# A two-sequence hybrid encoder layer on one core: head by depth block, last products reordered, final scaling on GpSimd's queue

## The chip, the cores and the metric

The kernel runs on one core of a Trainium2 chip. The metric is the device time of one execution in microseconds, as a median over runs. The engines are named as in the profile: PE is TensorE's matmul, PEld its weight load, DVE VectorE, ACT ScalarE, POOL GpSimd, SP SyncE, which issues most transfers. A "q" behind an engine's name (SPq, POOLq) means its sequencer, for issues of transfers.

## The reference

Two inputs, a prompt of 512 tokens and a sample of 1024 tokens, of width 2048, pass the same layer with shared weights, everything in float32:

```python
def mixer_layer(x, norm_g, w_in, w_dw, b_dw, ln_g, ln_b, w_pw, sink, w_out):
    h = rms_norm(x, norm_g)
    z = h @ w_in                      # widths: val, glu, gate 1024 each, q 1024, k and v 256, gate 1024
    c_val, c_glu, c_gate, q, k, v, a_gate = jnp.split(z, split_points, axis=-1)
    ...
    conv_out = conformer_conv(c_val, c_glu, w_dw, b_dw, ln_g, ln_b, w_pw) * jax.nn.silu(c_gate)
    attn_out = banded_sink_attention(q, k, v, sink) * jax.nn.silu(a_gate)
    mix = jnp.concatenate([conv_out, attn_out], axis=-1) @ w_out
    return x + mix

def encoder(x, ...):
    x = mixer_layer(x, ...)           # one layer
    return rms_norm(x, final_norm_g)  # the final scaling spoken of here
```

The convolution has 31 taps over 1024 channels, the attention 8 heads of 128 with a band of one block of 128 to each side. `y_p` is the prompt's output, `y_s` the sample's.

## The kernel before

**Products.** Every large product is made of 128x512 matmuls in float32 with a reduced multiplier. An operand is split into a high part (a copy by ACT, L487) and a remainder (a difference by DVE, L488); three matmuls, high by high, high by remainder and remainder by high, make one product. The tiles of weights so split are `hl` (three buffers), their loads `raw` (three buffers of 512 KB), the tokens so split `t`. A weight tile needs 12 matmuls. Larger units are multiplied in seven block products in Strassen's manner (P1 to P7, over sums of blocks of tokens and of weights) instead of eight.

**Order.** The program is written as one stream on TensorE. After each few matmuls (`tick`) lanes of side work are advanced by a credit in time: each side job is a generator that yields the time that it is worth. A yielded number so sets how soon its next part is emitted and where it stands in the in-order queues of ACT, DVE and the transfers. `w_prep` prepares the next weight tiles ahead of the products.

**Head.** The very first unit (`Plain`, matmuls on L329) multiplies directly in eight steps: a half of the tokens, a half of the depth, and one of two columns of weights. Before it, SP loads four weight pieces of 512 KB for the halves of depth, and 8 tiles of x, halved in tokens. `token_sum` (L490 on ACT) splits x, with the norm's gain `norm_g`; `first_sums` goes through them.

**Last stage, from about 1932 us.** Two things run side by side. On TensorE the prompt's output product (`last_run`, L1762 for all but the last product, L1721 for the last): two column halves c, in each the seven products in the order P1 P2 P6 P5 P7 P3 P4 (`ALONE`), each over four weight tiles; two token blocks share a bank pair, so there are four blocks b of 128 rows. `tap` adds a product's bank into the rows (L1663). When one quarter of a block's row is complete (after P2, P7, P3, P4), `complete` squares it with a running sum on ACT (L1672) and multiplies it by the final gain on DVE (L1673). At a row's fourth quarter the root and its reciprocal follow (L681, L682), then four scalings of 128x512 by that row's number, in turn on DVE and ACT (L1688, L1686), and four stores of 256 KB into `y_p` (L1689). The second column half's rows of x and gains are loaded after the fourth product (`load_columns(1)`).

Beside it, a side job (`finish`) finishes the sample: for each half of the tokens it sums squares over the columns, takes the root, spreads the number over the partitions (L699, copied out on L1366); after both halves it goes over 16 blocks of 128 rows in `y_d`: loads one (even ones as one 128x1024 tile `f`, odd ones as two 128x512 tiles `p`, of which there are four), scales it on DVE (L1374) and stores it into `y_s` (L481). Loads are issued three blocks ahead; all its transfers are on SP's queue, where the weights' loads are, too. Accumulating transfers earlier in the kernel (L478) are those of GpSimd's queue.

Of the kernel before, what the change touches and what calls it, by code (L numbers as in the profile page):

```python
# [57 lines left out]
DIRECT = ("P1", "P2", "P3")  # L58
TURNS = ("P1", "P2", "P5", "P6", "P7", "P3", "P4")
# [240 lines left out]
class Plain(Unit):  # L300


    STEPS = [(0, 0, 0), (0, 0, 1), (0, 1, 0), (0, 1, 1), (1, 0, 0), (1, 0, 1), (1, 1, 0), (1, 1, 1)]

    def preps(self):
        self.raws = [self.e.raw_tile() for _ in range(2)]
        return [Prep(None, None) for _ in range(2)]

    def load_half(self, c, k):
        self.e.nc.sync.dma_start(self.raws[c][:, k], self.w[c][:, k * HALF : (k + 1) * HALF, :])  # L310

    def make_half(self, c, k):
        e = self.e
        t = e.hl[c] if c in e.hl else e.hl_tile()
        e.parts(t[:, 0, k], t[:, 1, k], self.raws[c][:, k])
        e.hl[c] = t
# [4 lines left out]
    def product(self, step, late):  # L321
        e, nc = self.e, self.e.nc
        t, k, c = self.STEPS[step]
        if k == 0:
            self.bank[t, c] = e.PS("abac"[2 * t + c], [W])
        acc, hl, toks = self.bank[t, c], e.hl[self.at[c]], e.T[f"A{t + 1}{k + 1}"]
        for j in range(HALF):
            for q, (l, r) in enumerate(((0, 0), (0, 1), (1, 0))):
                nc.tensor.matmul(  # L329
                    acc,  # L330
                    hl[:, l, k, j, :],
                    toks[j][:, r],
                    start=k == 0 and j == 0 and q == 0,
                    stop=k == 1 and j == HALF - 1 and q == 2,
                )
            if j == 0:
                for fn in late:
                    fn()
                if step >= 4:
                    e.w_prep(3 if step < 7 else 4)  # L340
                e.turn_over()
            e.tick(3 * MM)
        if step >= 6:
            e.hl.pop(self.at[c])
        for fn in self.after.get(step, ()):
            fn()
        return [lambda: e.urgently(self.tap, (t, c))] if k else []
# [60 lines left out]
class Encoder:  # L408
# [119 lines left out]

    def constants(self):
        nc, a = self.nc, self.a  # L530

        def load(key, shape):
            t = self.const.tile([P] + shape, F32, name="c_" + key)
            nc.sync.dma_start(t, a[key])
            return t

        self.norm_g = load("norm_g", [ND])
        self.norm_n = self.const.tile([P, ND], F32, name="norm_n")
        nc.vector.tensor_scalar(self.norm_n, self.norm_g, -1.0, None, ALU.mult)
# [3 lines left out]
        nc.vector.tensor_copy(self.ones_r, self.ones)  # L543

        def rest():
# [162 lines left out]
class Sequence:  # L708
# [64 lines left out]
    def first_sums(self, x):  # L773

        e, nc = self.e, self.e.nc
        col = lambda t, k: t[:, k : k + 1]
        for t in range(2):
            for k in range(2):
                for j in range(HALF):
                    self.token_sum(f"A{t + 1}{k + 1}", 0, j, x[j + k * HALF][:, t * W : t * W + W])  # L780
                yield
# [429 lines left out]
class Mix:  # L1211
# [128 lines left out]
    def finish(self):  # L1340
# [3 lines left out]
        def load(o):  # L1344
            if o >= ND:
                return
            if o % 2:
                ys = [e.PT("p", NP, [W]) for _ in range(2)]
                for t, y in enumerate(ys):
                    nc.sync.dma_start(y, self.y_d[o][:, t * W : t * W + W])  # L1350
            else:
                ys = [e.F([TS])]
                nc.sync.dma_start(ys[0], self.y_d[o])
# [4 lines left out]
        yield LOAD  # L1358
        for t in range(2):
            s = self.sv[:, t]  # L1360
            v = e.column_sums(s, W, 1.0 / D, RMS_EPS)
            r = e.small(NB)
            e.rsqrt(r, v, NB)
            yield S7
            ps = yield from e.spread(r, room=e.F)
            nc.scalar.activation(s, ps, AF.Copy)  # L1366
            yield 1000
        rb = self.sv.rearrange("p t n -> p (t n)")
        for o in range(ND):
            ys = held.popleft()  # L1370
            n = TS // len(ys)
            for t, y in enumerate(ys):
                cols = slice(t * n, t * n + n)
                nc.vector.scalar_tensor_tensor(y, y, e.fin_g[:, o : o + 1], rb[:, cols], ALU.mult, ALU.mult)  # L1374
                e.store(self.out[o][:, cols], y)
            load(o + 3)
            yield 2000
# [126 lines left out]
class LastPost(Post):  # L1504
# [90 lines left out]
    def last_weights(self):  # L1595
# [28 lines left out]
        for c in range(2):  # L1624
            for name in ALONE:
                for m in self.PAIRS:
                    self.place[c, name, m] = len(preps)
                    preps.append(one(c, name, m, c == 1 and name == ALONE[-1]))
# [36 lines left out]
    def complete(self, b, c, odd):  # L1665
# [7 lines left out]
        nc.vector.tensor_tensor(y, y, self.gain[c, odd], ALU.mult)  # L1673
# [5 lines left out]
        if n == 3:  # L1679
# [3 lines left out]
            for j in range(D // W):  # L1683
                y = self.column(self.rows[b], j)
                if j % 2:
                    nc.scalar.activation(y, y, AF.Identity, scale=r)  # L1686
                else:
                    nc.vector.tensor_scalar(y, y, r, None, ALU.mult)  # L1688
                nc.sync.dma_start(self.out[b * P : (b + 1) * P, j * W : (j + 1) * W], y)  # L1689
# [4 lines left out]
        "P7": ((1, 1),), "P3": ((0, 1),), "P4": ((1, 0),),  # L1694
# [4 lines left out]
    def tap(self, c, name, t, acc):  # L1699
        h, odd = self.ADDS[name][0]  # L1700
        self.add(2 * h + t, c, odd, acc)

    def last_run(self, at):
        e, nc = self.e, self.e.nc
        self.seen = {}
        tags = [{"P1": ("a", "a"), "P2": ("b", "c"), "P5": ("s", "s")}, {"P1": ("pt", "pv"), "P2": ("b", "c"), "P5": ("s", "s")}]
        pending = []
        step = 0
        for c in range(2):
            bank = [None] * 3  # L1710
            for name in ALONE:
                n = BANK[name]
                if name in FRESH:
                    bank[n] = [e.PS(tag, [W]) for tag in tags[c][name]]
                acc = bank[n]
                end = c == 1 and name == ALONE[-1]

                def products(t, m, i, part):
                    first, last = m == self.PAIRS[0] and i == 0, m == self.PAIRS[-1] and i == 1
                    for q, (x, l) in enumerate(self.PASSES):  # L1720
# [4 lines left out]
                            start=name in FRESH and first and q == 0,  # L1725
                            stop=name in LAST and last and q == 2,
# [24 lines left out]
                before = c == 1 and name == ALONE[-2]  # L1751
                for n, m in enumerate(self.PAIRS):
# [5 lines left out]
                    for i in range(2):  # L1758
                        for q, (x, l) in enumerate(self.PASSES):
                            for t in range(2):  # L1760
# [5 lines left out]
                                    start=name in FRESH and first and q == 0,  # L1766
                                    stop=name in LAST and last and q == 2,
# [6 lines left out]
                if step == 3:  # L1774
                    self.load_columns(1, e.F)
                step += 1
                done, pending = pending, []
                for t in range(2):
                    finished(t)
                for args in done:  # L1780
                    e.urgently(self.complete, *args)


def encoder(ctx, tc, a):
# [27 lines left out]
    def first():  # L1812
        x = [e.F([TS]) for _ in range(NF)] + [e.A([TS], F32)]
        part = lambda k, t: e.nc.sync.dma_start(x[k][:, t * W : t * W + W], sample.xT[k][:, t * W : t * W + W])
        for k in range(2):
            plain.load_half(0, k)
            for j in range(HALF):
                part(j + k * HALF, 0)
            plain.load_half(1, k)
# [3 lines left out]
        e.w_load(3)  # L1823
        sums = sample.first_sums(x)
        x = None
        for k in range(2):
            plain.make_half(0, k)
            next(sums)
            plain.make_half(1, k)
        next(sums)  # L1830
        next(sums)
        e.ready = 2
        plain.after[1] = [lambda: next(sums)]
# [239 lines left out]
```

## Time and profile before

| | |
|---|---|
| three runs | 2105.66, 2110.05, 2110.88 us, median 2110.05 |
| the profiled execution | 2105.98 us, of it span 2104.2 us |
| TensorE clock granted, mean | 0.995 |
| PE busy | 2062.6 us (98%), 9234 matmuls |
| DVE busy | 1752.5 us (83%) |
| ACT busy | 1042.7 us (50%) |
| POOL busy | 77.2 us (4%) |
| transfers | 494.53 MB, 235 GB/s over the span |

A timeline row has the start within the span, the duration, the engine, the line, the operation and its tiles (out<-in), and how many like it follow in a row; a bracket gives the idle time before it and what ended it. A row of waits has the engine, the tile and the line that waited, the tile and line that it waited for, then microseconds in total, times, and the longest. A group's row has the count, the busy time, the mean of one in ns, and the idle time before them. A row of transfers ends with count, size of one and microseconds from issue to landing.

### The profile page before, as it was taken

The numbers are of one execution on the slowest core, as the hardware profiler recorded it, in microseconds if no ns is written. First come the engines' busy times: TensorE is split into PE (matmuls) and PEld (weight loads), VectorE is DVE, ScalarE is ACT, GpSimd is POOL, SyncE is SP. The second block draws the span as 40 slices with busy tenths as digits, with TensorE's granted clock in tenths as the row PEclk, the third lists the DMA queues.
The fourth block names the chain that finished last, engine by engine and source line by source line (L and its number), as shares of the span: only waits on it lengthen the run. The fifth ranks groups of instructions, "written<-read, shape, count | busy, mean of one in ns | idle before, by whom it ended". The sixth has DMA issues, their size and how long they took to land.

```text
span 2104.2 us, 26927 instructions
## 1 busy us (share of the span) xinstructions
PE 2062.6 (98%) x9234; PEld 1693.9 (81%) x9234; DVE 1752.5 (83%) x2855; ACT 1042.7 (50%) x1682; POOL 77.2 (4%) x92
## 2 busy tenths in 40 slices
PE   8999999999999999999999999999999999999996
PEld 7878888888877888788888888887888888888885
DVE  8658798998899999999566777766799988899777
ACT  6476435333454444644455777336554343455444
POOL 0001110000001111100000000000000000000000
PEclk9999999999999999999999999999999999999998
DMA  8888887865577667954556555996689898677798
GB/s 283 305 290 248 204 216 229 292 206 171 179 230 191 171 168 180 274 162 150 160 174 188 175 180 188 318 333 208 234 286 302 280 328 286 212 263 269 250 311 308
DMA packets 248025, 494.53 MB, mean 235 GB/s; under 512 B 23248, under 2 KB 83024, under 8 KB 247888
## 3 DMA queue, kind: packets, MB, share of 16 engines
q1 hardware_dynamic: 235216, 469.74, 67.1%
q0 software_dynamic: 12672, 23.07, 6.9%
q8 instruction: 72, 1.18, 0.2%
q14 instruction: 65, 0.53, 0.1%
HBM read 331.77 MB, written 160.96 MB: 234 GB/s over the span
## 4 chain that ended last, share of the span: by engine, by line
PE 76%; DMA 9%; DVE 9%; issue 3%; ACT 2%; SPq 0%; POOL 0%; ACTq 0%; DVEq 0%; POOLq 0%
PE a L198 21%; PE a L632 13%; PE c L198 10%; PE c L632 6%; PE b L632 6%; PE b L198 5%; DVE hl L488 2%; PE pv L1145 2%; PE s L1116 2%; PE s L198 2%; PE a L1762 2%; DMA raw<-wsum_P 1%; PE pt L1150 1%; DMA f<-x_s 1%; PE s L1762 1%
## 5 line engine op out<-in xcount | busy, mean ns | idle before, releaser
L198 PE MATMUL a<-t,hl 128*128 128x512 f32 x2640 | 633.3, 391 | 8.1 <-ACT u L224 3.7
L198 PEld LDWEIGHTS a<-t,hl 128*128 128x128 f32 x2640 | 493.5, 188 | 115.6 <-ACT u L224 6.9
L487 ACT ACTIVATE hl<-raw 128x1024 fp32r<-128x1024 f32 (+1 forms) x356 | 324.1, 911 | 435.8 <-DVE raw L140 93.3
L488 DVE TENSOR_TENSOR hl<-raw,hl 128x1024 fp32r<-128x1024 f32 (+1 forms) x356 | 369.0, 1037 | 148.4 <-ACT hl L487 147.0
L632 PE MATMUL a<-t,hl 128*128 128x512 f32 x1344 | 329.7, 395 | 0.3 <-DVE hl L488 0.3
L198 PE MATMUL c<-t,hl 128*128 128x512 f32 x1320 | 320.8, 391 | 0.2
L198 PEld LDWEIGHTS c<-t,hl 128*128 128x128 f32 x1320 | 248.0, 188 | 53.3 <-ACT g L224 0.9
L632 PEld LDWEIGHTS a<-t,hl 128*128 128x128 f32 x1344 | 249.5, 189 | 50.8 <-DVE hl L488 0.7
L1000 DVE SCALAR_TENSOR_TENSOR f<-f,c_w_dw,f 128x512 f32<-128x512 f32 x248 | 174.9, 745 | 0.3
L632 PE MATMUL c<-t,hl 128*128 128x512 f32 x672 | 165.5, 394 | 0.0
L963 DVE SCALAR_TENSOR_TENSOR f<-f,c_w_dw,f 128x512 f32<-128x512 f32 x232 | 163.5, 743 | 1.7 <-ACT f L958 1.7
L632 PE MATMUL b<-t,hl 128*128 128x512 f32 x672 | 163.5, 392 | 0.2 <-DVE hl L488 0.2
L198 PE MATMUL b<-t,hl 128*128 128x512 f32 x660 | 160.0, 390 | 0.0
L632 PEld LDWEIGHTS b<-t,hl 128*128 128x128 f32 x672 | 124.9, 188 | 25.4 <-DVE hl L488 0.7
L632 PEld LDWEIGHTS c<-t,hl 128*128 128x128 f32 x672 | 125.1, 189 | 24.4
L198 PEld LDWEIGHTS b<-t,hl 128*128 128x128 f32 x660 | 123.7, 188 | 25.5
L992 DVE SCALAR_TENSOR_TENSOR f<-f,w_both,f 128x512 f32<-128x512 f32 x120 | 89.7, 748 | 1.8
L395 ACT ACTIVATE hl<-raw 128x1024 fp32r<-128x1024 f32 x44 | 46.5, 1056 | 61.2 <-PE a L632 23.6
L224 ACT ACTIVATE u<-a 128x512 f32<-128x512 f32 x82 | 48.6, 593 | 56.1 <-PE a L198 52.4
L224 ACT ACTIVATE g<-a 128x512 f32<-128x512 f32 x78 | 46.3, 593 | 59.1 <-PE a L198 53.9
L1130 ACT ACTIVATE p<-p,tiny 128x384 f32<-128x384 f32 (+1 forms) x96 | 54.6, 570 | 38.0 <-DVE tiny L1127 27.7
L487 ACT ACTIVATE a<-pt 128x512 fp32r<-128x512 f32 x64 | 38.0, 593 | 65.7 <-PE pt L1150 65.5
(332 smaller groups left out, 2562.0 us busy)
## 6 DMA issues: line engine op xcount, KB each, us to landing
raw<-w_in SPq DMA_DIRECT2D x171, 512.0 KB, 5.0
raw<-wsum_P SPq DMA_DIRECT2D x32, 512.0 KB, 4.9
raw<-w_out SPq DMA_DIRECT2D x31, 512.0 KB, 5.2
raw<-w_pw SPq DMA_DIRECT2D x24, 512.0 KB, 4.5
raw<-w_last SPq DMA_DIRECT2D x24, 512.0 KB, 5.3
wsum_P<-raw SPq DMA_DIRECT2D x47, 256.0 KB, 3.5
f<-x_s SPq DMA_DIRECT2D x16, 512.0 KB, 6.7
a<-sum_S SPq DMA_DIRECT2D x24, 256.0 KB, 6.0
```

The lines of the kernel that those rows point to most:

```text
L198: nc.tensor.matmul(acc, hl[:, l, o, j, :], toks[j][:, r], start=name in FRESH and j == 0 and q == 0, stop=name in LAST and j == HALF - 1 a ...
L224: nc.scalar.activation(t, bank, AF.Copy)
L395: e.nc.scalar.activation(t[:, 0], raw, AF.Copy)
L487: nc.scalar.activation(hi, x, AF.Copy)
L488: nc.vector.tensor_tensor(lo, x, hi.bitcast(F32), ALU.subtract)
L632: nc.tensor.matmul(job.acc[0], hl[:, l, kk // HALF, kk % HALF, :], r, start=i == 0 and p == 0, stop=i == nk - 1 and p == 2,)
L963: nc.vector.scalar_tensor_tensor(t, h[:, j : j + T], w(j), t, ALU.mult, ALU.add)
L992: nc.vector.scalar_tensor_tensor(m0, odd[:, j : j + H], both(j), m0, ALU.mult, ALU.add)
L1000: nc.vector.scalar_tensor_tensor(out, d[:, j : j + H], w(2 * j + k), out if j else m0, ALU.mult, ALU.add)
L1116: nc.tensor.matmul(ps[:, 0:n], qs[:, x, h], k[y][:, keys], start=p == 0, stop=p == 2)
L1130: nc.scalar.activation(p[:, 0:n], p[:, 0:n], AF.Exp, bias=nm[:, h : h + 1], accum_out=l[:, h : h + 1])
L1762: nc.tensor.matmul(acc[t], self.toks[name, m][:, x, i, t * P : (t + 1) * P], parts[i][l].rearrange("p a b -> p (a b)"), start=name in FRES ...
```

## The change

Four parts:

1. Head: the first unit runs through the depth block by block (a quarter of the depth for both columns in each of eight steps), its weights are loaded in pieces of one or three blocks between the x tiles, splits follow in the same order, and 16 small matmuls of 128x128 ones stand ahead of it (`warm`). `norm_n` is computed later.
2. `finish`: the sample's statistics are taken over all 1024 tokens in one pass, and both halves are spread directly behind one another. Loads and stores of the scaling are issued by GpSimd instead of SP; the yield between blocks is 5000 instead of 2000.
3. Last column half: the products go P1 P2 P6 P5 P3 P7 P4 (`ENDS`). P7 is added to two quarters there, and P4 is summed in banks of its own. The first block pair's rows are so complete after P3, the second's after P4. `complete` is emitted in the midst of the next product. `load_columns(1)` comes after the sixth product instead of the fourth.
4. Last scaling of a row: the fourth quarter isn't multiplied by the gain first; gain and row number go in at once (`scalar_tensor_tensor`), other quarters on ACT or DVE as before, and each row block is stored in two pieces of 512 KB instead of four of 256 KB.

```diff
+ENDS = (ALONE, ("P1", "P2", "P6", "P5", "P3", "P7", "P4"))
...
 class Plain(Unit):
-    STEPS = [(0, 0, 0), (0, 0, 1), (0, 1, 0), (0, 1, 1), (1, 0, 0), (1, 0, 1), (1, 1, 0), (1, 1, 1)]
+    STEPS = [(t, q) for t in range(2) for q in range(HALF)]
...
+    def load_some(self, c, k, j0=0, j1=HALF):
+        self.e.nc.sync.dma_start(self.raws[c][:, k, j0:j1], self.w[c][:, k * HALF + j0 : k * HALF + j1, :])
...
     def product(self, step, late):
+        t, quarter = self.STEPS[step]
...
+        for n in range(2):
+            i = 2 * quarter + n
+            k, j = divmod(i, HALF)
+            toks = e.T[f"A{t + 1}{k + 1}"]
+            for c in range(2):
+                acc, hl = self.bank[t, c], e.hl[self.at[c]]
+                for q, (l, r) in enumerate(((0, 0), (0, 1), (1, 0))):
+                    nc.tensor.matmul(acc, hl[:, l, k, j, :], toks[j][:, r], ...)
...
+    def warm(self):
+        ps = self.PS("pt", [P])
+        for _ in range(16):
+            self.nc.tensor.matmul(ps, self.ones_r, self.ones_r, start=True, stop=True)
...
     def finish(self):
...
-                    nc.sync.dma_start(y, self.y_d[o][:, t * W : t * W + W])
+                    nc.gpsimd.dma_start(y, self.y_d[o][:, t * W : t * W + W])
...
+        rb = self.sv.rearrange("p t n -> p (t n)")
+        v = e.column_sums(rb, TS, 1.0 / D, RMS_EPS)
+        r = e.small(2 * NB)
+        e.rsqrt(r, v, 2 * NB)
+        yield S7
         for t in range(2):
-            s = self.sv[:, t]
-            v = e.column_sums(s, W, 1.0 / D, RMS_EPS)
-            r = e.small(NB)
-            e.rsqrt(r, v, NB)
-            yield S7
-            ps = yield from e.spread(r, room=e.F)
-            nc.scalar.activation(s, ps, AF.Copy)
+            ps = yield from e.spread(r[:, t * NB : t * NB + NB], room=e.F)
+            nc.scalar.activation(self.sv[:, t], ps, AF.Copy)
             yield 1000
...
-                e.store(self.out[o][:, cols], y)
+                nc.gpsimd.dma_start(self.out[o][:, cols], y)
             load(o + 3)
-            yield 2000
+            yield 5000
...
     def complete(self, b, c, odd):
-        nc.vector.tensor_tensor(y, y, self.gain[c, odd], ALU.mult)
+        if n < 3:
+            nc.vector.tensor_tensor(y, y, self.gain[c, odd], ALU.mult)
...
+            for h in range(2):
+                other, last = (self.blocks(self.rows[b], h, o) for o in (1 - odd, odd))
+                nc.scalar.activation(other, other, AF.Identity, scale=r)
+                if h == c:
+                    nc.vector.scalar_tensor_tensor(last, last, r, self.gain[c, odd], ALU.mult, ALU.mult)
                 else:
-                    nc.vector.tensor_scalar(y, y, r, None, ALU.mult)
+                    nc.vector.tensor_scalar(last, last, r, None, ALU.mult)
+                nc.sync.dma_start(self.out[b * P : (b + 1) * P, h * half : (h + 1) * half], self.rows[b][h])
...
-        "P7": ((1, 1),), "P3": ((0, 1),), "P4": ((1, 0),),
+        "P7": ((1, 1), (1, 0)), "P3": ((0, 1),), "P4": ((1, 0),),
...
-                if step == 3:
+                    if n == 1:
+                        for args in pending:
+                            e.urgently(self.complete, *args)
+                        pending.clear()
+                if step == 5:
                     self.load_columns(1, e.F)
```

More of the change, by code (lines that the diff above doesn't have):

```diff
@@ L1624, in last_weights @@
         for c in range(2):
-            for name in ALONE:
+            for name in ENDS[c]:
                 for m in self.PAIRS:
                     self.place[c, name, m] = len(preps)
-                    preps.append(one(c, name, m, c == 1 and name == ALONE[-1]))
+                    preps.append(one(c, name, m, c == 1 and name == ENDS[c][-1]))
         return preps
@@ L1699, in tap @@
     def tap(self, c, name, t, acc):
-        h, odd = self.ADDS[name][0]
+        (h, odd), *more = self.ADDS[name]
         self.add(2 * h + t, c, odd, acc)
+        if c:
+            for h, odd in more:
+                self.add(2 * h + t, c, odd, acc)
     def last_run(self, at):
@@ L1710, in last_run @@
             bank = [None] * 3
-            for name in ALONE:
+            for name in ENDS[c]:
                 n = BANK[name]
-                if name in FRESH:
+                fresh, closing = name in tags[c], name in LAST or c == 1 and name == "P7"
+                if fresh:
                     bank[n] = [e.PS(tag, [W]) for tag in tags[c][name]]
                 acc = bank[n]
-                end = c == 1 and name == ALONE[-1]
+                end = c == 1 and name == ENDS[c][-1]
                 def products(t, m, i, part):
@@ L1724, in products @@
                             part[l].rearrange("p a b -> p (a b)"),
-                            start=name in FRESH and first and q == 0,
-                            stop=name in LAST and last and q == 2,
+                            start=fresh and first and q == 0,
+                            stop=closing and last and q == 2,
                             skip_group_check=True,
@@ L1750, in last_run @@
                     continue
-                before = c == 1 and name == ALONE[-2]
+                before = c == 1 and name == ENDS[c][-2]
                 for n, m in enumerate(self.PAIRS):
@@ L1765, in last_run @@
                                     parts[i][l].rearrange("p a b -> p (a b)"),
-                                    start=name in FRESH and first and q == 0,
-                                    stop=name in LAST and last and q == 2,
+                                    start=fresh and first and q == 0,
+                                    stop=closing and last and q == 2,
                                     skip_group_check=True,
@@ L1814, in first @@
         part = lambda k, t: e.nc.sync.dma_start(x[k][:, t * W : t * W + W], sample.xT[k][:, t * W : t * W + W])
[L1815 to L1819, printed above, removed]
+        plain.begin()
+        for k in range(2 * HALF):
+            half, j = divmod(k, HALF)
+            if j == 0:
+                plain.load_some(0, half, 0, 1)
+            part(k, 0)
+            if j == 0:
+                plain.load_some(1, half, 0, 1)
+                plain.load_some(0, half, 1)
+            if j == 1:
+                plain.load_some(1, half, 1)
         for k in range(2 * HALF):
@@ L1823, in first @@
         e.w_load(3)
+        e.warm()
         sums = sample.first_sums(x)
         x = None
-        for k in range(2):
-            plain.make_half(0, k)
+        for half in range(2):
+            for j in range(HALF):
+                if j == 0:
+                    plain.make_some(0, half, 0, 1)
+                next(sums)
+                if j < 2:
+                    plain.make_some(1 - j, half, j, HALF if j else 1)
+                if j == 1:
+                    plain.make_some(1, half, 1)
+        e.nc.vector.tensor_scalar(e.norm_n, e.norm_g, -1.0, None, ALU.mult)
+        for k in range(2 * HALF):
             next(sums)
-            plain.make_half(1, k)
-        next(sums)
-        next(sums)
         e.ready = 2
-        plain.after[1] = [lambda: next(sums)]
+        plain.after[3] = [lambda: next(sums)]
         plain.after[5] = [lambda: e.T.pop("A21")]
```

72 lines of the change are left out of this document (30 added, 42 removed).

## The prediction

> **What bounds the kernel now.** I read the page first, then the timeline of the head and of the tail, then the windows, groups and waits of the last stage, which begins at about 1932 us.
>
> ```profile
> span 2104.2 us, 26927 instructions
> PE 2062.6 (98%) x9234; PEld 1693.9 (81%) x9234; DVE 1752.5 (83%) x2855; ACT 1042.7 (50%) x1682; POOL 77.2 (4%) x92
> q1 hardware_dynamic: 235216, 469.74, 67.1%
> PE 76%; DMA 9%; DVE 9%; issue 3%; ACT 2%; SPq 0%; POOL 0%; ACTq 0%; DVEq 0%; POOLq 0%
> ```
>
> TensorE is busy for 98% of the span, and the chain of waits runs 76% over it. The change alters no number of large matmuls, so time can come only from the two ends and from TensorE's stalls; and it can be lost where TensorE, now nearly unbroken, is made to wait. The order of instructions between about 60 and 1930 us is the same in both kernels, so I count nothing there.
>
> ```profile
> 6.31 5.84 PE L329 MATMUL a<-t,hl 128*128 128x512 f32 x12 [6.31 <-ACT t L490]
> 13.58 0.72 ACT L490 ACTIVATE t<-a,c_norm_g 128x512 fp32r<-128x512 f32 x1
> 17.88 2.88 PE L329 MATMUL b<-t,hl 128*128 128x512 f32 x12
> 20.60 2.88 PE L329 MATMUL a<-t,hl 128*128 128x512 f32 x12
> 27.51 1.22 DVE L488 TENSOR_TENSOR hl<-raw,hl 128x1024 fp32r<-128x1024 f32 x1
> 31.48 2.88 PE L198 MATMUL a<-t,hl 128*128 128x512 f32 x12
> 10.00:15.00 5.00, 5.00 (x18) 3.93 (x17) 4.57 (x7) 4.68 (x8) 0.00 (x0) 1.00 1.05 395
> 20.00:25.00 5.00, 5.00 (x24) 4.14 (x23) 5.00 (x8) 5.00 (x10) 0.00 (x0) 1.00 0.73 245
> ```
>
> Head: the first matmul starts at 6.31, and the first twelve take 5.84 us where a later twelve follow one another in 2.72 (17.88 to 20.60). In the columns of a window (length, then busy time of PE, PEld, DVE, ACT, POOL, the clock, DMA share, GB/s) the transfers run at 395 GB/s, the highest rate of these views, and from 20 us on DVE is full.
>
> ```profile
> 2087.65 0.74 DVE L1374 SCALAR_TENSOR_TENSOR p<-p,c_final_norm_g,f 128x512 f32<-128x512 f32 x1
> 2091.66 0.68 DVE L1663 TENSOR_TENSOR f<-pv,f 128x512 f32<-128x512 f32 x1
> 2092.43 0.63 ACT L1672 ACTIVATE g<-f 128x512 f32<-128x512 f32 x1
> 2095.16 0.16 DVE L682 RECIPROCAL tiny<-tiny 128x1 f32<-128x1 f32 x1 [0.27 <-ACT tiny L681]
> 2096.75 0.71 ACT L1686 ACTIVATE f<-f,tiny 128x512 f32<-128x512 f32 x1
> 2097.98 1.28 SPq L1689 DMA_DIRECT2D y_p<-f  x2
> 2099.32 0.64 SPq L481 DMA_DIRECT2D y_s<-p  x1
> y_p<-a SPq DMA_DIRECT2D x8, 256.0 KB, 3.3
> 2083.30 5.61 PE L1721 MATMUL pv<-t,t 128*128 128x512 f32 x24
> PE pt L1762 <- DVE hl L488: 0.7, 1, 0.7
> PE pt L1721 <- ACT t L487: 0.7, 1, 0.7
> ```
>
> Tail: the last matmuls run from 2083.30 for 5.61 us, to 2088.9. Only 2.8 us later DVE adds their sum (2091.66), because scaling of y_s and other rows' work stand ahead of it; squares, root and reciprocal reach 2095.3, the last scaling 2097.5, the stores are issued until 2099.96, and the span ends at 2104.2: 15.3 us after the last matmul. Two waits of 0.7 us hold TensorE itself in the last two products.
>
> **The change part by part.**
>
> *Head.* Weights come in smaller pieces between the x tiles, so matmuls can follow each x tile, and 16 small matmuls run while nothing else can. The bytes up to the eighth x tile stay the same, so it can't arrive earlier. It is split at 13.58 to 14.30, a remainder on DVE follows (some 0.7), and the last six of the first 48 matmuls need 1.4: these 48 would end at 17 to 18 instead of 20.60. I take 2.7 us (0 to 3.5). What could give it back is the weight stream behind, with DVE full from 20 us on: the remainder that begins at 27.51 ends at 28.73 and its matmuls begin at 31.48, 2.75 us later, so just about this gain fits; if that cover weren't there, the gain would be nothing. A rule is weighed here: the Trainium skill, "TensorE: Matmul & The Clock Gate", Part 1, says that the clock doubles once TensorE has been busy through one window of about 3.4 us. The 5.84 against 2.72 us agrees with it; by it the small matmuls could take up to 3.1 us off the first twelve, where the arrival of x lets through no more than my 2.7.
>
> *Tail.* The last half goes P1 P2 P6 P5 P3 P7 P4: rows of two of the four blocks are complete after P3, two products before the end, so half of y_p goes out under matmuls (its price if that cover were gone: the two blocks' stores back behind the last matmul). No scaling of y_s is left there. For the very last block I take from the rows above: an addition begun 0.1 us after the last matmul (0.7), square with its sum 0.8, root and reciprocal 0.6, two scalings that overlap 1.2, two stores of 512 KB issued (0.5 each): issued by +4.4. The 256 KB row lands in 3.3 us; 1 MB at the end lands, as an estimate between once and twice that, 5 us after it. So the span ends at +9.4 instead of +15.3: 5.9 gained (4 to 7). The two stalls of 0.7 go too, and I count 1.7 with the refill around them (0 to 2): P4 gets banks of its own and DVE is freer there. The gain factor folded into the last scaling takes four products off DVE, all in the tail, in the chain above. Sum of the gains: 2.7 + 5.9 + 1.7 = 10.3 us.
>
> *Statistics at once, and the scaling's queue.* The scaling (L1374) needs the statistics of both token halves. Those of the second now come at 2001.18:
>
> ```profile
> 1952.31 0.58 ACT L1366 ACTIVATE f<-s 128x512 f32<-128x512 f32 x1
> 2001.18 0.58 ACT L1366 ACTIVATE f<-s 128x512 f32<-128x512 f32 x1
> L1374 DVE SCALAR_TENSOR_TENSOR p<-p,c_final_norm_g,f x16: 741/744/753, 1954.1 to 2087.6; 128x512 f32<-128x512 f32 x16
> L1374 DVE SCALAR_TENSOR_TENSOR f<-f,c_final_norm_g,f x8: 1274/1281/1286, 2002.6 to 2084.1; 128x1024 f32<-128x1024 f32 x8
> L488 DVE TENSOR_TENSOR hl<-raw,hl 128x1024 fp32r<-128x1024 f32 x50 | 61.0, 1222 | 18.6 <-ACT hl L487 18.2
> ACT hl L487 <- PE a L1762: 14.5, 9, 1.7
> DVE p L1374 <- DMA p<-y_d: 6.6, 5, 2.0
> ```
>
> So 24 scalings are spread over 133 us today. In the new order of instructions all of them stand on DVE ahead of the weight remainder (L488's kind, 1222 ns) of the third tile of P4 in the first column half: 18 weight tiles from about 1953 on, 18 x 2.72 = 49 us. This is where the change can cost. The same 49 us today, for all instructions and for the scalings alone, the fullest transfers of the stage, and the pieces:
>
> ```profile
> 1953.00:2002.00 49.00, 49.00 (x221) 40.50 (x220) 35.90 (x54) 22.40 (x31) 0.00 (x0) 1.00 0.78 254
> 1953.00:2002.00 49.00, 2.98 (x4) 1.00 0.78 254
> 2070.00:2080.00 10.00, 10.00 (x45) 8.26 (x44) 8.72 (x16) 5.42 (x11) 0.00 (x0) 1.00 0.96 345
> p<-y_d SPq DMA_DIRECT2D x12, 256.0 KB, 4.7
> y_s<-p SPq DMA_DIRECT2D x16, 256.0 KB, 5.3
> y_s<-f SPq DMA_DIRECT2D x8, 512.0 KB, 6.9
> f<-x_p SPq DMA_DIRECT2D x4, 512.0 KB, 6.2
> L478 POOL DMA_DIRECT2D g<-part_q x16 | 14.7, 920 | 64.1 <-DVE g L244 56.4 <-DMA q_d<-u 6.9 <-ACT g L224 0.8
> ```
>
> First DVE: 35.90 now, less 2.98, plus all scalings (16 x 0.744 + 8 x 1.281 = 22.2) is 55.1 us of work in 49, 6 us too much. TensorE has a reserve: ACT often waits until TensorE lets go of a weight buffer (14.5 us in 9 waits), so of three buffers two stand ready, 2 x 2.72 = 5.4 us. DVE alone would cost under 1 us.
>
> Then the transfers: 254 GB/s x 49 us = 12.4 MB now. Loads of 2.6 MB for the second column half (four of the x_p rows and two gains) move two products later, out of the stretch. Of the y_s traffic (8.4 MB each way) 20 of 24 scalings come in, 14.0 MB. That is 23.8 MB: at the 395 GB/s of the head 60.3 us, 11.3 beyond 49, and after the reserve 5.9 us of stall. At the 345 GB/s of the stage's fullest stretch it is 69.0 us, a stall of 14.6. The lower bound is nothing: the scalings might simply run late at no one's cost, if the scheduler's order left the weights room. I take 5.9, since 395 is what the queues reached when nothing held them back, and this stretch would be such a one. The reserve counted away, the stall comes because DVE works in order: a scaling that waits for its y_d tile (six and a half us of such waits already today, at a third of the density) holds the weight remainders queued behind it, and TensorE waits for those.
>
> Moving 48 issues to GpSimd's queue: POOL issues one in 0.92 us, 44 us over the stretch's 49 and beside nothing else, since all its other transfers lie earlier; and SP's weight loads no longer stand behind a y_s store that waits for DVE. I count this at 0 (from 1 gained to the price of the second rival). In sum −10.3 + 5.9 = −4.4 us: 2105.98 − 4.4 = 2101.6 on the profiled execution's own time (span 2104.2 and 1.8 around it). The median of the runs shown, 2110.05, lies 4.07 above that execution, so the forecast for a median is 2105.6. No change within 0.3% means here within 6.3 us, about what can be told apart.
>
> **The rivals.** *The cost is hidden (0.18).* The scalings find gaps on DVE and in the transfers, and the weights keep their reserve. For it: transfers were at 0.78 of their share in this stretch, and SP gets free. Against it: the 23.8 MB. It gives −10.3, 2099.7.
>
> *GpSimd's chain of buffers becomes the bound (0.24): slower.* The odd columns use four p tiles. Each runs: issue 0.92, load 4.7, scaling 0.74, issue 0.92, store 5.3, together 12.6 us; four tiles give one p scaling in 3.15 us, and 16 of them 50 us, just the stretch. On POOL every load waits for the store that frees its tile, and the stores queued behind wait with it, and DVE, in order, waits for the loads. The waits for y_d in the rows above speak for it; that y_s flowed at today's pace with no loss of TensorE speaks against it. The net turns slower than 6.3 from a stall of 16.6: 16 p scalings in 71 us, 4.4 us each, that is load and store together in 15.2 us instead of 10.0. At 15.5 the stall is 18 us, the net +7.7, the time 2117.8. The Trainium skill, "DMA: Bandwidth & Descriptors", in "Queues, rings and completion order", says that a DMA engine takes packets of the queues in turn; in "Rules for kernel authors", that more issuing engines bring no bandwidth. By these rules a y_d load is shared half and half with the weights' queue, and its 4.7 us could reach 9.4, which is past the point named. No trace here shows two full queues at once.
>
> *The ends give little (0.08).* The head's gain is used up by the full DVE until 55 us and the tail's stalls come back elsewhere: −5.9 + 5.9 = 0, 2110.
>
> **How the numbers follow.** The forecast's case (0.50) has by its bounds a range of its own, 2098 to 2112. Of it 0.22 lies beyond −6.3, 0.27 within, 0.01 above. The hidden case is faster, the chain slower, the last one mostly the same (0.07, and 0.01 slower). That makes 0.40, 0.34 and 0.26. The range reaches from 2096 (2099.7, less the larger bounds of head and tail) to 2118, the slower rival's time.
>
> **What would show it.** In the new profile: the first 48 matmuls over by 18 us; last matmul to end of span near 9.4; no scaling after about 2010; stalls of TensorE on DVE's weight remainders in the first column half, 6 us in sum, with DVE waiting for y_d by more than 11; GB/s near 395 there. If TensorE's pitch there is unbroken, the hidden case holds; if the sum of the stalls is over 16 us with POOL's loads landing after 8 us or more, the chain does. A head that still ends its 48 matmuls after 20 us, or a tail above 12, would show those steps wrong.

## The result: slower, by the queue that the forecast counted at nothing

The changed kernel takes 2125.2 us beside 2108.0 of the kernel before, a ratio of 1.0091 [1.0068, 1.0114]. The forecast was 2105.6, with a range up to 2118. Its profiled execution has 2127.4 us. These are lines of its page:

```profile
span 2125.6 us, 26999 instructions
PE 2075.9 (98%) x9250; PEld 1699.6 (80%) x9250; DVE 1751.3 (82%) x2851; ACT 1042.6 (49%) x1685; POOL 103.6 (5%) x140
q1 hardware_dynamic: 227728, 452.96, 64.3%
q0 software_dynamic: 17536, 39.85, 9.0%
```

16.8 MB have moved from q1 to q0, GpSimd's queue. TensorE's busy time grew by 13.3 us; 3.7 of it are the 16 small matmuls. About 6.5 come from 13.7 us at half clock in the last stage (below), where matmuls take nearly twice as long (in the head, three in a row take 1.48 us at first and 0.84 later); I have not placed the rest. Where the 21.4 us of the span lie follows from a comparison of TensorE's 9234 matmuls one by one, the 16 small ones left out: matmul 8500 (about 1922 us) starts 2.6 us later than in the kernel before, matmul 8900 is 29.0 later, the last one ends 27.6 later (2116.5), and the end of the span gains 6.2 back. The 2.6 us were there before the last stage, in a part whose order is the same in both; I give them no cause. The rest is the first column half of the last stage. In windows of the changed kernel (columns as above):

```profile
1953.00:2002.00 49.00, 42.12 (x171) 33.48 (x170) 31.35 (x42) 16.20 (x20) 11.97 (x22) 0.93 0.89 316
2002.00:2051.00 49.00, 38.04 (x148) 28.96 (x147) 34.52 (x41) 17.11 (x26) 10.90 (x20) 0.93 0.87 305
1970.00:1980.00 10.00, 7.14 (x25) 5.49 (x24) 8.74 (x10) 1.60 (x2) 2.71 (x5) 0.83 0.70 229
1990.00:2000.00 10.00, 8.31 (x29) 6.46 (x30) 6.11 (x7) 3.63 (x4) 3.28 (x6) 0.83 1.03 419
```

In the two stretches of 49 us, 171 and 148 matmuls are counted instead of 221 and 218, and every engine has idle time. The transfers stand at 316 and 305 GB/s in the mean, but they come in bursts: the two rows of 10 us have 229 and 419 GB/s, at shares of 0.70 and 1.03. So no engine is full, and the transfers are full only at times: things wait for one another. The waits of the last stage (engine, tile, line, what it waited for; total, times, longest), and in the last row one of the kernel before:

```profile
ACT hl L496 <- DMA raw<-wsum_P: 27.1, 9, 6.5
POOL p L1363 <- DMA y_s<-p: 23.6, 6, 7.0
DVE p L1386 <- DMA p<-y_d: 11.4, 3, 8.1
DVE f L1386 <- DMA f<-y_d: 9.9, 4, 5.4
PE a L1781 <- DVE hl L497: 7.7, 3, 6.0
POOL f L1366 <- DMA y_s<-f: 7.6, 3, 2.8
PE s L1781 <- DVE hl L497: 6.4, 3, 2.9
PE a L1781 <- ACT hl L496: 2.8, 1, 2.8
ACT hl L487 <- DMA raw<-wsum_P: 24.9, 15, 2.8
```

GpSimd waits for a store to land before it can load into the tile, DVE waits for the load, TensorE for the weight remainder behind it on DVE: 14.1 us of TensorE's waits end so. The wait of 2.8 us has another end: TensorE waits for ACT's copy of a weight tile, and ACT for the tile's own load. ACT's waits for such loads are not much longer in sum than in the kernel before, but the longest is 6.5 us instead of 2.8. One stall of the first kind in the timeline:

```profile
2019.74 0.54 POOL L1366 DMA_DIRECT2D f<-y_d  x1 [2.83 <-DMA y_s<-f]
2028.18 1.28 DVE L1386 SCALAR_TENSOR_TENSOR f<-f,c_final_norm_g,f 128x1024 f32<-128x1024 f32 x1 [5.42 <-DMA f<-y_d]
2029.38 1.28 DVE L1675 TENSOR_TENSOR a<-s,a 128x512 f32<-128x512 f32 x2
2030.58 1.21 DVE L497 TENSOR_TENSOR hl<-raw,hl 128x1024 fp32r<-128x1024 f32 x1
2031.85 1.65 PE L1781 MATMUL a<-hl,t 128*128 128x512 f32 x3 [6.03 <-DVE hl L497]
```

The load is issued at 2019.74, after a wait of 2.83 us for a store to land; it lands at 2028.1 itself. DVE idles 5.42 us in front of the scaling, although two additions and a weight remainder stand ready behind it; TensorE stands for 6.03 us and then runs at half clock for 6.8 us.

The tail, in contrast, is as forecast:

```profile
2115.68 0.84 PE L1740 MATMUL a<-t,t 128*128 128x512 f32 x3
2116.56 0.69 DVE L1675 TENSOR_TENSOR f<-a,f 128x512 f32<-128x512 f32 x1 [0.75 <-PE a L1740]
2120.18 0.70 ACT L1699 ACTIVATE f<-f,tiny 128x512 f32<-128x512 f32 x1
2120.91 0.33 SPq L1704 DMA_DIRECT2D y_p<-f  x1
```

From the last matmul's end, 2116.5, to the end of the span there are 9.1 us (forecast 9.4, before 15.3). The head is not as forecast:

```profile
1.32 3.67 PE L541 MATMUL pt<-ones_r 128*128 128x128 f32 x16 [1.32 <-DVE ones_r L555]
5.40 0.80 PE L337 MATMUL a<-t,hl 128*128 128x512 f32 x1 [0.40 <-ACT t L499]
8.33 0.79 PE L337 MATMUL a<-t,hl 128*128 128x512 f32 x1
11.56 1.48 PE L337 MATMUL a<-t,hl 128*128 128x512 f32 x3
14.61 0.72 ACT L499 ACTIVATE t<-a,c_norm_g 128x512 fp32r<-128x512 f32 x1 [0.34 <-DMA a<-xT_s]
20.75 0.84 PE L337 MATMUL a<-t,hl 128*128 128x512 f32 x3
```

The first 48 matmuls are over at 20.75, where the kernel before had 20.60.

### The profile page after: what moved, and what is told of

The parts are those of the page before. It is cut to its first block, busy times and chain, and to the rows that moved or that the text cites. A ratio compares the mean times of both kernels' runs of the same rounds, so it can differ in the third digit from the quotient of the medians.

```text
span 2125.6 us, 26999 instructions
## 1 busy us (share of the span) xinstructions
PE 2075.9 (98%) x9250; PEld 1699.6 (80%) x9250; DVE 1751.3 (82%) x2851; ACT 1042.6 (49%) x1685; POOL 103.6 (5%) x140
## 5 line engine op out<-in xcount | busy, mean ns | idle before, releaser
L496 ACT ACTIVATE hl<-raw 128x1024 fp32r<-128x1024 f32 (+3 forms) x360 | 324.4, 902 | 453.0 <-DVE raw L141 98.6
L497 DVE TENSOR_TENSOR hl<-raw,hl 128x1024 fp32r<-128x1024 f32 (+3 forms) x360 | 370.2, 1029 | 161.7 <-ACT hl L496 160.0
```

Source lines behind the costliest of these rows:

```text
L496: nc.scalar.activation(hi, x, AF.Copy)
L497: nc.vector.tensor_tensor(lo, x, hi.bitcast(F32), ALU.subtract)
```

## The experiments

All compare with the kernel before on the same chip. "Stall" is what TensorE's starts between 1950 and 2100 us lie apart beyond the pitch of 0.2267 us (12 matmuls in 2.72 us), summed over the gaps above 0.26 us, half clock included. "Places" are the weight tiles of the last stage (of some 51) between which the 24 scalings stand in DVE's order.

| | scaling on | places | stall, us | ratio to before |
|---|---|---|---|---|
| before | SP | 9–51 | 2.4 | 1 |
| changed | POOL | 9–27 | 27.0 | 1.0091 [1.0068, 1.0114] |
| e1 old scaling | SP | 9–46 | 16.5 | 1.0034 [1.0024, 1.0044] |
| e2 e1, on POOL | POOL | 9–42 | 24.1 | 1.0067 [1.0048, 1.0087] |
| e3 changed, on SP | SP | 9–48 | 6.0 | 0.9988 [0.9974, 1.0002] |
| e4 half the bytes | POOL | 9–30 | 15.7 | 1.0028 [1.0015, 1.0041] |
| e5 no stores | POOL | 9–27 | 2.7 | 0.9961 [0.9949, 0.9974] |
| e6 scaling by GpSimd | POOL | none on DVE | 18.6 | 1.0046 [1.0033, 1.0058] |
| e7 e1, rows early | SP | 9–51 | 3.3 | 0.9991 [0.9982, 0.9999] |
| e8 e3, rows early | SP | 9–48 | 1.9 | 0.9979 [0.9968, 0.9990] |
| e9 e7, on POOL | POOL | 9–42 | 23.6 | 1.0064 [1.0046, 1.0083] |
| e10 loads POOL, stores SP | both | 9–34 | 17.8 | 1.0041 [1.0027, 1.0056] |
| e11 head only | SP | 9–51 | 1.7 | 0.9997 [0.9984, 1.0010] |
| e12 e8, old head | SP | 9–48 | 2.5 | 0.9976 [0.9963, 0.9990] |
| e13 changed, spread | POOL | 13–46 | 16.1 | 1.0027 [1.0013, 1.0042] |
| e14 e12, spread | SP | 13–50 | 11.3 | 1.0004 [0.9993, 1.0015] |
| e15 e13, dense | POOL | 13–31 | 19.9 | 1.0067 [1.0046, 1.0089] |

**The parts: e1, e2, e3.** e1 takes `finish` back whole, e2 then moves its transfers, e3 takes back only the queue:

```diff
 e1: finish() as in the kernel before; all else as changed
 e2: e1, and
-                nc.sync.dma_start(ys[0], self.y_d[o])       (likewise the p tiles and the stores)
+                nc.gpsimd.dma_start(ys[0], self.y_d[o])
 e3: the changed kernel, and
-                nc.gpsimd.dma_start(self.out[o][:, cols], y) (likewise the loads)
+                nc.sync.dma_start(self.out[o][:, cols], y)
```

> The changed kernel with the sample's statistics and scaling as before (per half, SP's queue, yield 2000); head and last products stay changed. Where the loss sits in the scaling pulled forward, the 26 us of stalls in the first column half are gone and the 6.2 us of the tail stay: about 2102 us. Where the new order of products or the later load of the second half's rows costs, the time stays above 2108.

> As e1, but the scaling's loads and stores on GpSimd's queue. In the order of instructions on DVE the 24 scalings stand between the 9th and the 42nd weight tile of the stage (e1: 9th to 46th; changed kernel: 9th to 27th). If GpSimd's chain of buffers costs by itself, it shows here: 2110 us or more, with stalls of TensorE between 2000 and 2080. If the packing costs and the queue doesn't, it equals e1 within 2 us.

> The changed kernel with the scaling's transfers back on SP's queue, statistics at once and yield 5000 kept. The scheduler then puts 12 scalings between the 9th and the 21st weight tile, the others from the 29th to the 48th. If GpSimd's queue is the cause: 2102 us. If the packing is: two thirds of the density for two thirds of the stretch, stalls of 5 to 10 us instead of 26, 2107 to 2112 us.

e3 gave 2103.0 us, 22 less than the changed kernel: the queue in the code is what made it slow, with the order that comes with it (places 9–48 instead of 9–27). e1 gave 2112.8, against my theory. Its loss is one stall of 13.2 us at the start of the second column half. In its timeline:

```profile
2029.27 2.51 SPq L1658 DMA_DIRECT2D f<-x_p  x4
2036.15 0.69 DVE L1676 TENSOR_TENSOR f<-pt,f 128x512 f32<-128x512 f32 x1 [0.45 <-DMA f<-x_p]
2036.99 1.62 PE L1782 MATMUL pt<-hl,t 128*128 128x512 f32 x3 [12.82 <-DVE f L1676]
```

The second half's rows, which the change loads two products later, are issued at 2029 only, on SP's queue behind weights and two loads of the scaling; the addition into them, and the bank behind it, wait. They use f tiles, as the scaling does; that these tiles are what makes them so late is argued, not shown. That loading these rows late asks for a scaling pulled forward wasn't in the forecast. e2 gave 2118.6, slower than e1 as its queue theory said; its stalls are others (most of TensorE's wait there is for weight remainders).

**Bytes, chain, DVE's order: e4, e5, e6.** e4 moves half of each tile, e5 leaves out the stores, e6 has GpSimd do the scaling:

```diff
 e4: loads, stores: [:, t * W : t * W + W]  ->  the first half of these columns; scaling twice on that half
 e5:
+                if o == ND - 1:
                     nc.gpsimd.dma_start(self.out[o][:, cols], y)
 e6:
-                nc.vector.scalar_tensor_tensor(y, y, e.fin_g[:, o : o + 1], rb[:, cols], ALU.mult, ALU.mult)
+                nc.gpsimd.tensor_tensor(y, y, rb[:, cols], ALU.mult)
+                nc.gpsimd.tensor_scalar(y, y, e.fin_g[:, o : o + 1], None, ALU.mult)
```

> The changed kernel with half of each scaling tile's columns left out of load and store (half of y_s isn't written) and the kept half scaled twice, so that DVE has about the same work in the same order and the same number of transfers of half the size. 8.4 MB of the stretch's 23.8 fall away. If the rate of the transfers is the bound, the stalls fall from 26 to under 6 us: about 2104 us. If the chain of issue, load, scaling and store is the bound by its latencies, which hardly fall with size, the time stays at 2117 us or more. If DVE's own work is the bound, it stays too, with DVE full between 1953 and 2040.

> The changed kernel without the stores of y_s but for the last row block's (that part of the output is left out). The same order on DVE and 7.9 MB less, about as many bytes as the experiment with half the columns takes away, which left 14 us of stalls. If bytes alone count, 14 us stay here too: about 2112 us. If it is the chain of buffers (a load waits for the store that frees its tile, and DVE for the load), its longest link is cut: stalls under 5 us, 2100 to 2103 us.

> The changed kernel with the scaling done by GpSimd in two operations (by the row number, by the gain) instead of one on DVE; same transfers, same queue, a longer chain. DVE has no instruction left that waits for y_d. If the stalls come because such a waiting scaling holds the weight remainders behind it in order, they fall to under 6 us (about 2103 us), however late the scaling runs. If the weights' own transfers starve beside y_s, the stalls stay at 15 us or more, with ACT waiting for raw tiles: 2113 us or more.

e4 and e5 take nearly the same bytes away. e4 (2111.8 us) keeps 15.7 us of stall, between the two figures expected; e5 (2096.9) keeps 2.7. The store that must land before its tile is loaded again is the link that counts, and bytes count by how long they make that link: with half the bytes the p tiles' stores landed in 4.9 us instead of 7.0. In e5, between 1953 and 2002 us, DVE and the transfers were fuller than in any of the others and TensorE still ran. The second row is e12's (below, everything on SP's queue):

```profile
1953.00:2002.00 49.00, 48.27 (x210) 38.93 (x209) 43.60 (x50) 20.50 (x26) 8.60 (x16) 1.00 0.95 344
1953.00:2002.00 49.00, 49.00 (x217) 40.54 (x216) 39.38 (x45) 22.49 (x30) 0.00 (x0) 1.00 0.91 319
```

So a rate of 344 GB/s in this stretch doesn't stall TensorE by itself, and with one queue TensorE is unbroken at 319, where the changed kernel had 316. e6 missed its 2103 us: it gave 2113.6. Up to 2050 us its stalls are 11 us instead of 26 (by 50 us stretches, 2.9 and 8.4 instead of 10.5 and 15.6), so a part of them does come from DVE's order; but GpSimd's compute slowed DVE, as the groups of DVE and the timeline show:

```profile
L497 DVE TENSOR_TENSOR hl<-raw,hl 128x1024 fp32r<-128x1024 f32 x49 | 74.7, 1537 | 36.6 <-ACT hl L496 36.5
2063.21 3.68 DVE L497 TENSOR_TENSOR hl<-raw,hl 128x1024 fp32r<-128x1024 f32 x1 [1.71 <-ACT hl L496]
2063.24 2.49 POOL L1386 TENSOR_TENSOR p<-p,f 128x512 f32<-128x512 f32 x2
2065.71 4.93 POOL L1387 TENSOR_SCALAR p<-p,c_final_norm_g 128x512 f32<-128x512 f32 x2
```

The mean is 1537 ns instead of 1222, with single ones up to 3962. So e6 can't say how much DVE's order alone is worth. Nor does it rule out its other case, weights that starve beside y_s: 18.6 us of stall in all and 2113.6 us are what it foretold there, and ACT waited 50.4 us for raw tiles, where it waited 37.3 in the changed kernel.

**Rows early: e7, e8; the queue alone: e9, e10.** e7 and e8 are e1 and e3 with the rows of the second half loaded where the kernel before loads them; e9 is e7 with the scaling's transfers on GpSimd's queue; e10 is the changed kernel with the stores alone on SP's.

```diff
 e7, e8, e9:
-                if step == 5:
+                if step == 3:
                     self.load_columns(1, e.F)
```

> The kernel of e1 (old statistics and scaling, new head and last products) with the second column half's rows loaded after the fourth product, as in the kernel before, instead of after the sixth. If e1's stall of 13 us comes from these rows, which wait for tiles that the scaling holds, it goes: the tail's 6 us remain, 2098 to 2101 us beside 2105 of before. If it is the scaling as such, it stays near 2112.

> The kernel of e3 (statistics at once, scaling's transfers on SP's queue) with the second column half's rows loaded after the fourth product. The scalings then stand spread from the 9th to the 48th weight tile without a gap. If density is what costs, the 6 us of stalls of e3 fall to 2 or 3: 2099 us. If tiles held by these rows slow the scaling, it becomes slower than e3: 2105 us or more.

> The kernel of e7 (2103.3 us) with the scaling's loads and stores on GpSimd's queue, nothing else changed; the scalings then stand between the 9th and 42nd weight tile instead of the 9th and 51st. If GpSimd's queue is harmless as long as the scaling isn't packed, 2098 to 2104 us. If its in-order chain (a load waits for a store to land, what is behind waits too) stalls DVE and through it TensorE also in a spread order, 2110 us or more, with waits of POOL for landed stores above 10 us.

> The changed kernel with only the stores of y_s moved back to SP's queue; loads stay on GpSimd's. A load that waits for its tile then holds no store behind it. Scalings stand from the 9th to the 34th weight tile. If loads and stores that hold one another on one in-order queue make the chain, stalls fall from 26 to under 8 us: 2101 to 2106 us. If the density of transfers does it, in 25 tiles instead of 18 they fall by about a third only: 2115 us.

e7's stall is gone, so e1's was that of the rows. It gave 2103.3 us, less gain than expected; its tail is 12.2 us, since scalings of y_s stand in it again. e8 is faster than both kernels, 2099.5 us. e9 differs from e7 by the queue in the code, and costs 15 us; its places end at 42 instead of 51. GpSimd's waits in e9:

```profile
POOL p L1363 <- DMA y_s<-p: 35.2, 10, 8.2
POOL y_s L1388 <- DVE f L1387: 32.5, 4, 25.6
```

With the scalings spread over 33 places the queue still waits for landed stores ten times, and four times at a store for its scaling on DVE; whatever stands behind on the queue waits, too. e10's figure of 17.8 us lies where the density theory put it (2113.1 us beside 2115 expected): to free the loads of the stores in front of them on the queue wasn't enough, since the load still waits for its tile's store to land (43.1 us in 5 waits).

**Head: e11, e12.** Before with the new head alone; e8 with the old one.

> The kernel before with the new head alone. By the prediction's step 2.7 us less than before; by the profiles so far (first 48 matmuls over between 18.9 and 21.5 us in eight profiles with the new head, 20.6 in the one of before) 0 to 1 us, not told from no change.

> The kernel of e8 (2099.5 us, ratio 0.9979) with the old head. If the head gives nothing, it equals e8 within 1.5 us; if it gives the 2.7 us of the prediction, it is 2102 us.

The head gives nothing that can be told from no change: 0.9997 in e11, and e12, with the old head, is at 2098.0 us no slower than e8. e11's interval alone would still let 2.7 us through (0.9987). e12 has 0.9976 where such a head, taken out of e8 (0.9979), would have left 0.9992. e12 is the fastest whole kernel found: statistics at once, scaling on SP's queue, the new order of products and the new tail, rows early, old head.

**Queue or place on DVE: e13, e14, e15.** The yield of 5000 didn't spread the scalings, since the scheduler puts an instruction where its engine has room by its own account. A tie behind the last instructions emitted makes the yield count:

```diff
+                        e.mark()
                         e.tick(6 * MM)
...
 rows early in all three (step == 3, as in e7)
...
-            yield 5000
+            yield 4000        (e13 on GpSimd's queue, e14 on SP's; e15: 1500, on GpSimd's)
```

> The changed kernel on GpSimd's queue, with the second half's rows loaded early, a yield of 4000 instead of 5000, and the side job's steps tied behind the last DVE and ACT instructions emitted so far, so that the 24 scalings stand on DVE from the 13th to the 46th weight tile. If the order on DVE is what fails with GpSimd's queue (scalings put ahead of their loads), the stalls go: 2096 to 2101 us. If the queue itself costs, also with room on DVE, it stays near the 2113 to 2119 us of e9 and e10.

> The kernel of e12 (SP's queue, rows early, old head, 2098 us) with the same tie and yield 4000: scalings from the 13th to the 50th weight tile. By either theory no stalls, 2095 to 2099 us; against e13 it gives the price of the queue at nearly the same order.

> The kernel of e13 with a yield of 1500: scalings from the 13th to the 31st weight tile, as dense as in the changed kernel but started four tiles later. If density with in-order waits costs, 2112 us or more; if only the start ahead of the loads did, 2100 us.

They gave 2112.1, 2107.3 and 2120.6 us. On the same queue, spread costs 1.0027 and dense 1.0067: how densely the scalings stand matters. Their places on DVE and the density of their transfers change together here, so these two runs don't part them. At nearly the same spread, GpSimd's queue has 1.0027 and SP's 1.0004, with intervals that just touch: the queue matters too, by some 5 us (the heads differ as well, which e11 and e12 put at nothing). e14 missed its 2095 to 2099 us, and e13 lies nearer to its second case than to its first. Each of the two has a stall that I hadn't foreseen; in e14:

```profile
2056.41 0.75 DVE L1374 SCALAR_TENSOR_TENSOR p<-p,c_final_norm_g,f 128x512 f32<-128x512 f32 x1 [1.69 <-DMA p<-y_d]
2057.08 1.28 DVE L1663 TENSOR_TENSOR f<-s,f 128x512 f32<-128x512 f32 x2
2057.91 2.47 PE L1769 MATMUL s<-hl,t 128*128 128x512 f32 x5 [5.65 <-DVE f L1663]
```

In the new order P3 follows P5 and adds into P5's banks (s), so it can't begin before P5's additions; these stand behind a scaling that waits for its tile. Here 6.0 us, in e13 8.3, so 2.3 of the 5 us between the two queues lie in this one place.

## Why the prediction failed

*The step that failed is the costing of the queue and of the stretch behind it.* The prediction put 48 issues on GpSimd at 0 and took the stall at 5.9 us from a rate: 23.8 MB at 395 GB/s beyond 49 us, less a reserve. The transfers reached that rate at times (419 GB/s in one window of 10 us) but did not hold it, 316 and 305 in the mean. The scalings, which were to be over by about 2010, ran from 1957.1 to 2034.9, and the stall was 27.0 us less some 1 in the second half. The second rival had the right mechanism (loads that wait for landed stores, DVE in order behind them), with 18 us and a chance of 0.24. Its own point of decision didn't hold, though: it named load and store together at 15.2 us for a p tile, and they landed in less. The first two rows are of the whole last stage; the others hold for 1953 to 2035 us, while the scaling runs, four of the changed kernel and then two of the kernel before:

```profile
y_s<-p POOLq DMA_DIRECT2D x16, 256.0 KB, 7.0
p<-y_d POOLq DMA_DIRECT2D x12, 256.0 KB, 5.8
q0 software_dynamic: 4096, 14.16, 47.0%
q1 hardware_dynamic: 3439, 12.52, 44.0%
raw<-wsum_P SPq DMA_DIRECT2D x13, 512.0 KB, 7.1
raw<-w_last SPq DMA_DIRECT2D x7, 512.0 KB, 6.7
raw<-wsum_P SPq DMA_DIRECT2D x17, 512.0 KB, 4.9
raw<-w_last SPq DMA_DIRECT2D x12, 512.0 KB, 5.1
```

12.8 us were enough. The likely reason is that the f tiles hang on the same in-order queue, so that a wait for either kind stops both; GpSimd's waits above are of both kinds, but no run parts them. The weights' own transfers became slower while the scaling ran, 7.1 and 6.7 us instead of 4.9 and 5.1, and the two queues had nearly the same share of the transfer engines' time, 47.0 and 44.0%. That agrees with the rule that I weighed there, the sharing of packets between queues in the Trainium skill, "DMA: Bandwidth & Descriptors", "Queues, rings and completion order". Some weight loads were also issued late, since DVE let go of the raw tiles late: in the stall shown above the remainder ran at 2030.58 only, and the next load into its tile was issued at 2031.82. Slow weights are not the whole cause: in e4 they landed in 4.4 and 4.6 us over the same stretch, and 15.7 us of stall stayed. How much of the 26 us they make is open. The issues were cheaper than I took them, 0.54 us instead of 0.92; the time didn't go by them.

*The reserve of 5.4 us* was counted once against the whole lag. DVE's seven waits for y_d tiles (21.3 us in all, the longest 8.1) met it again and again, as I read it when the buffers had just been emptied. And of four pauses of TensorE above 2.5 us three (3.2, 3.2 and 6.4) ended in half clock, the one of 2.6 didn't: three stretches from 1973, 1990 and 2031 us on, 13.7 us in all, which the forecast didn't count.

*The tail* was right: 6.2 us gained for 5.9. *The two stalls of 0.7* went, but the order P5, P3 brought one of its own of about 1 us (P3 waits for P5's additions); the lag fell from 29.0 to 27.6 us there, so the 1.7 us became about 1.4.

*The head* was mis-sized: 2.7 us became 0. I let the last x tile set the end, with six matmuls behind it. It was split at 14.61 to 15.33, but 36 of the 48 matmuls began at 11.56 only, the first of them at the long pitch, and needed until 20.75: TensorE was the bound, not the tile. And the small matmuls did not bring the clock forward: the granted clock on record in the profiles goes to full between 8.4 and 14.7 us in the fourteen with them, at 9.5, 11.8 and 12.9 us in the three without.

*What the forecast missed altogether:* the later load of the second half's rows ties the scaling to the change of order. With the scaling as before it costs 13 us of stall and 9 of time (e1 against e7).

How far DVE's order, and how far the slower turn of the queue alone, makes up the 22 us between e3 and the changed kernel isn't settled: e13 to e15 point to both, but the tie that spreads the scalings brought a stall of its own. The two queues also differ in kind (software_dynamic and hardware_dynamic in the profile's page), and no run put the scaling on a second queue of SP's kind. So that the queue in the code costs is shown (e3, and e9 against e7), and that it does so through the stores (e5, beside e4 with as many bytes less); the shares of the chain, of DVE's order and of the slower weights are not.

## What to carry to other kernels

Where loads and stores recycle few tiles, cost the loop by landing times per turn and by what each wait holds up on every in-order engine it passes, not by bytes over the best rate. A queue that looks free can hide its price in the scheduler's order: here the same code with its transfers on GpSimd's queue had its scalings in places 9–27 instead of 9–48, ahead of their data, and what stood behind them on DVE waited. Test a combined change by its parts in pairs: late rows cost 13 us of stall beside the scaling as before (e1), and hardly anything beside the early one on SP's queue (e3 against e8).

## What the hardware showed beside

DVE's 128x1024 difference has a mean of 1221 to 1223 ns in the last stage of the kernel before, the changed one, e2, e9, e10 and e13; in e6, where GpSimd computed beside it, the mean is 1537 and the longest 3962 ns. And 16 small matmuls of 3.67 us in a row were not followed by a full clock in the changed kernel until 13.7 us.
